# Attention's eight gated rows in two seven-product units, and w_o's first two rows split by operand

## The chip, the cores and the metric

The kernel runs on one core of a Trainium2 chip. The metric is device time in microseconds (us): the median of three runs of the kernel before is 2486.24 us (2486.18 to 2487.11). The engines are named as the profile names them: PE is TensorE (PEld its weight loads), DVE is VectorE, ACT is ScalarE, POOL is GpSimd, SP is SyncE, which here only issues DMAs. Each engine works through its own queue in order and waits at an instruction until what it needs is there.

## The reference

Two layers of an encoder trunk over 640 tokens (512 new ones, and 8 running streams of 16), width 1024. Each layer is a half feed-forward step, a mixer, and another half feed-forward step. The change touches the end of the mixer:

```python
g = jax.nn.sigmoid(g + b_gate)                 # 2 x 1024 gate columns of z = h @ w_in
g_conv, g_attn = jnp.split(g, 2, axis=-1)
y_conv, conv_new = _short_conv(cb, cc, cv, conv_prev, w_conv)      # 512 channels
y_attn, k_new, v_new = attn_fn(q, k, v)                            # 512 channels
m = g_conv * (y_conv @ w_conv_out) + g_attn * (y_attn @ w_attn_out)
return m @ w_o, conv_new, k_new, v_new         # added to x
```

`w_conv_out` and `w_attn_out` are 512 x 1024, `w_o` is 1024 x 1024. All of it is float32.

## The kernel before

Tensors lie transposed: 128 channels on the partitions, 640 tokens along the free side, in two halves of 320 (t1, t2). A "row" is 128 output channels. Every float32 product is made of three matmuls of a rounded type: an operand is split into a high part, cast by ACT, and a low part, the rest, subtracted by DVE (`whi`/`wlo` for weights, names ending in `hi`/`lo` for data); the matmuls are high x high, high x low, low x high.

Two ways of multiplying occur. The plain way (`product`, L448, `multiply`, L430): for each row, each 128-channel block of the input and each token half, three matmuls of 128 x 320. The seven-product way: input blocks are taken in even and odd pairs, and the output in two rows r and two token halves, so that a 2 x 2 by 2 x 2 block product needs seven products instead of eight, of mixed weights and mixed data. The data kinds are X11, X21, X22 (a block as it is) and T5, T7, N6, T4 (sums and differences of blocks); the weight kinds come from two slabs of 1024 columns and sums of their halves. The order is always X11, X21, N6, T5, T7, X22, T4, and N6, T7 and T4 add onto PSUM tile `a`, which is copied out between.

Weights come as 512 KB slabs from HBM on SP's queue, in the order that `mixer_order` (L115) writes, into three `raw` buffers. `source` (L301) makes a slab's mixed weights on DVE, `prep` (L350) issues the high casts on ACT two slabs ahead, `flush` (L366) the low subtractions on DVE; `slab` (L373) takes the next one, `quiet` takes it without preparing. A seven-product unit uses four such entries, from two slabs. For the third of them the sum of two halves is added by a DMA pair on POOL (`lend_one`, L277, tile `one`).

`outputs` (L1485) is the stage in question. PE, DVE and ACT run exactly in the order in which the code is written here (`manual_schedule`). It has:
- `gate_pair(m, at)` (L1506), "gates m": two gate rows by seven, 84 matmuls. `at` holds three places at which extra work of DVE and ACT can be put: before product X21, before T7 and before X22. The sigmoids are left to the next unit (`lates`, issued by `due`).
- `out(m, y)` (L1551): one plain row, 24 matmuls, then gating, and for attention rows the addition to `mm`.
- `rows(name, ms, y)` (L1617), "rows co": four rows by seven, 84 matmuls, with the gating in seven steps on DVE and the copies s1, s2, s5 out of PSUM on ACT. It is used for convolution rows 4 to 7.
- `mixed` (L1583) makes the mixtures of one pair of y blocks in place and splits them.

The order in a layer is gates 2, convolution rows 0 to 3 plain, gates 4, gates 6, rows co, and then four times: one gate pair (8, 10, 12, 14) and two plain attention rows (the products `py` from `ya`). `give` splits the merged rows m into high and low as operands of w_o, which follows: eight plain rows `po` of 48 matmuls, each added to x and passed to `ex.final`, which prepares the next feed-forward step.

PSUM has two accumulators of two banks (`acc`) and four of one bank (`att`) in this stage. Gate tiles come from a pool of four (`tmp`).

Of the kernel before, what the change touches and what calls it, by code (L numbers as in the profile page):

```python
# [126 lines left out]

# [66 lines left out]
def trunk(ctx: ExitStack, tc: tile.TileContext, xin, wst, small, pbias, samplebias, kcache, vcache, gfin,  # L196
# [24 lines left out]
    def acc(name):  # L221
        return banks["acc"].tile([P, 2, 512], F32, tag="acc", name=name)
# [7 lines left out]
    def tmp(name):  # L230
        return tp.tile([P, UW], F32, tag="t", name=name)[:, :T]

    def split(hi, lo, src):
        ACT.copy(hi, src)
        DVE.tensor_tensor(out=lo, in0=src, in1=hi.bitcast(F32), op=ALU.subtract)
# [1097 lines left out]
    def mixer(l, after):  # L1333
# [151 lines left out]
    def outputs(l, gp, X, st, cs, ycp, yas, sigmoid, gates):  # L1485
# [15 lines left out]
        def due():  # L1501
            for f in lates:
                f()
            lates.clear()

        def gate_pair(m, at):  # L1506
            n = f"{l}_{m}"
            pa, pb, pc = (att(f"q{i}{n}")[:, :HT] for i in "abc")
            u, g = gates[m], gates[m + 1] = tmp(f"g{n}"), tmp(f"g{n}_1")
            s0 = quiet()  # L1510
            block(pa, s0, 0, X11, every, True, True)
            ACT.copy(c1, pa)
# [9 lines left out]
            ACT.copy(u2, pa)  # L1522
# [42 lines left out]
            if post:  # L1565
                post()

        yc, ya, mo = [], [], []
        more = []
        yas_ = [yas[:, c, :] for c in range(CT)]  # L1570
# [5 lines left out]
        def give(ms):  # L1576
            for m in ms:
                mo.append(parts(hp, "h", f"m{l}_{m}", mm[m]))
# [4 lines left out]
        def mixed(i, y, z):  # L1583

            z = z.rearrange("p c (a b) -> p (c a) b", a=2)
            e1, e2, o1, o2 = (z[:, i] for i in range(4))
            add(e1, e1, e2, ALU.subtract)
            add(e2, o2, e2, ALU.subtract)
            for out, a in ((o2, e1), (o1, o2)):
                DVE.scalar_tensor_tensor(out=out, in0=a, scalar=-1.0, in1=out, op0=ALU.mult, op1=ALU.subtract)  # L1590
            yield
            hi, lo = (gp.tile([P, 3, HT], F32R, tag=f"x{i}{p}", name=f"x{p}{l}_{len(more)}") for p in ("hi", "lo"))
            ACT.copy(hi, z[:, 1:])
            more.append((hi, lo))
            yield
            low(lo, z[:, 1:], hi)
            yield
            hi, lo = (u[:, t2] for u in y[2 * i])
            ACT.copy(hi, e1)
            yield  # L1600
            low(lo, e1, hi)
            yield

        def take_even(c, src):
            y = tuple(gp.tile([P, T], F32R, tag=f"y{c}{i}", name=f"ya{l}_{c}{i}") for i in ("hi", "lo"))
            split(*(z[:, t1] for z in y), src[:, t1])
            ya.append(y)

        EXTRA = XT7, XT4, XN6

        def kind(y, i, k):
            if k in EXTRA:
                return tuple(z[:, EXTRA.index(k)] for z in more[i - 2])
            hi, lo = y[2 * i + (k in (X21, X22))]
            return tuple(z[:, t2 if k in (X22, XT5) else t1] for z in (hi, lo))

        def rows(name, ms, y, then=None):  # L1617

            n = f"{name}{l}_{ms[0]}"
            gs = [gates[m + (KT if name == "ao" else 0)] for m in ms]  # L1620
# [5 lines left out]
            def mul(ps, s, half, k, start):  # L1626
                for u in range(2):
                    for i in range(2):
                        kp = half * NP + 2 * u + i
                        wh, wl = (z[:, kp * P : (kp + 1) * P] for z in s)  # L1630
                        xh, xl = kind(y, i, k)
                        for j, (w, x_) in enumerate(((wh, xh), (wh, xl), (wl, xh))):
                            PE.matmul(ps[u], w, x_, start=start and i == 0 and j == 0,
                                      stop=i == 1 and j == 2, skip_group_check=True)
# [24 lines left out]
            mul(a, w, 0, XN6, False)  # L1659
            ACT.copy(s2, two(A))  # L1660
            gated(0, [s1[:, u] for u in range(2)], t1)
            mul(c, w, 1, XT5, True)
            for u in range(2):
                ACT.copy(s5[:, u], c[u])
# [11 lines left out]
            if then:  # L1676
                then()
# [8 lines left out]
        def total(m0, m1):  # L1686
            for m in range(m0, m1):
                add(mm[m], mm[m], gates[KT + m])

        none = lambda: None  # L1690

        def also(*fs):
            return lambda: [f() for f in fs]

        def going(z):
            return lambda: next(z)

        gate_pair(2, [none, none, lambda: take(yc, "yc", range(CT), ycs)])
        z = [mixed(i, yc, ycp[i]) for i in range(2)]
        out(0, yc, None, going(z[0]))  # L1700
        out(1, yc, None, also(going(z[0]), going(z[1])))
        out(2, yc, None, also(going(z[0]), going(z[1])))
        out(3, yc, None, going(z[1]))
        both = also(going(z[0]), going(z[1]))
        gate_pair(4, [both, both, none])
# [665 lines left out]
```

## Time and profile before

| | |
|---|---|
| median of 3 runs | 2486.24 us |
| profiled execution | 2487.08 us |
| its span, first to last instruction | 2485.3 us |
| PE busy | 2471.0 us, 99% |
| DVE busy | 2158.3 us, 87% |
| ACT busy | 1373.0 us, 55% |
| POOL busy | 317.4 us, 13% |
| granted clock of PE | 0.999 |

A row of the time-ordered view has start and duration in us, engine, source line, operation, tiles written and read, shapes and count; in brackets, how long the engine stood idle before it and what it waited for. Matmuls are pipelined, so a matmul lasts 0.31 us in such a row while the next starts 0.15 us later: the pace is read from starts. The same holds for DVE and ACT, whose next instruction starts up to 0.1 us before the last one's end if it does not need its result. A row of the waits has the waiting engine, tile and line, the releaser, the time in total, the number of waits, and the longest. Layer 0's gates, rows and w_o lie at about 635 to 833 us of the span, layer 1's at about 1867 to 2065 us.

### The profile page before, as it was taken

The page shows a single profiled execution, that of the slowest core. Times are in us where ns is not written, and L with a number is a line of the kernel's source. Part 1 is how long each engine was busy: PE and PEld are TensorE (multiplying, and loading weights), DVE is VectorE, ACT ScalarE, POOL GpSimd, SP SyncE. Part 2 cuts the span into 40 slices and gives each one's busy share as a digit, 9 for nine tenths or more (in the row PEclk, how much of TensorE's full clock was granted, in tenths as well). Part 3 has the DMA queues.
Part 4 walks back from the last instruction along what each step waited for, and adds up shares of the span by engine and source line. Part 5 has one row for each costly group of instructions (what it writes and reads, how often), then busy time and mean ns, then how long its engine had stood idle before and what let it go on. Part 6 is the DMA issues. An engine that isn't in the chain of part 4 may idle for free.

```text
span 2485.3 us, 43991 instructions
## 1 busy us (share of the span) xinstructions
PE 2471.0 (99%) x17288; PEld 2418.2 (97%) x17288; DVE 2158.3 (87%) x3587; ACT 1373.0 (55%) x2196; POOL 317.4 (13%) x479
## 2 busy tenths in 40 slices
PE   9999999999999999999999999999999999999999
PEld 8999999889999999999999999998999999999998
DVE  7999998888886899998799999988878769999997
ACT  6555556665554555555665555556645455555555
POOL 0111112211000001111001111121110000111111
PEclk9999999999999999999999999999999999999999
DMA  4443445335343334444334443453453333443444
GB/s 155 126 118 102 123 119 121 113 109 177 104 118 108 94 101 106 112 117 120 108 94 109 110 118 102 116 128 107 132 173 92 115 111 89 107 116 106 113 117 117
DMA packets 113072, 287.11 MB, mean 116 GB/s; under 512 B 12928, under 2 KB 52480, under 8 KB 112864
## 3 DMA queue, kind: packets, MB, share of 16 engines
q1 hardware_dynamic: 69552, 220.10, 28.0%
q0 software_dynamic: 42880, 63.94, 13.7%
q8 instruction: 135, 2.21, 0.4%
q14 instruction: 73, 0.60, 0.1%
q10 hardware_dynamic: 432, 0.25, 0.0%
HBM read 238.43 MB, written 7.94 MB: 99 GB/s over the span
## 4 chain that ended last, share of the span: by engine, by line
PE 92%; DVE 4%; ACT 2%; DMA 1%; issue 1%; SPq 0%; DVEq 0%; ACTq 0%; POOLq 0%
PE pab L458 12%; PE paa L458 11%; PE pcb L458 6%; PE daa L1143 6%; PE pca L458 5%; PE dab L1143 5%; PE po L434 5%; PE qa L458 4%; PE py L434 3%; PE pbb L458 3%; PE dca L1143 3%; PE pba L458 3%; PE dcb L1143 2%; PE ma_qk L458 2%; PE ma_cv L458 2%; PE pv L1770 2%
## 5 line engine op out<-in xcount | busy, mean ns | idle before, releaser
L363 ACT CAST whi<-raw 128x512 fp32r<-128x512 f32 (+1 forms) x573 | 500.4, 878 | 371.3 <-PE pbb L458 46.0
L368 DVE TENSOR_TENSOR wlo<-raw,whi 128x512 fp32r<-128x512 f32 (+1 forms) x573 | 574.4, 1005 | 135.9 <-ACT whi L363 132.1
L363 ACT CAST whi<-s 128x1024 fp32r<-128x1024 f32 (+1 forms) x160 | 151.6, 947 | 313.3 <-issue 111.4
L458 PE MATMUL pab<-xhib,whi 128*128 128x320 f32 x704 | 217.5, 309 | 0.0
L458 PE MATMUL pab<-xlob,whi 128*128 128x320 f32 x704 | 217.0, 308 | 0.0
L458 PE MATMUL pab<-xhib,wlo 128*128 128x320 f32 x704 | 217.0, 308 | 0.0
L458 PE MATMUL paa<-xhia,whi 128*128 128x320 f32 x640 | 197.7, 309 | 0.2 <-DVE ga L295 0.2
L458 PE MATMUL paa<-xhia,wlo 128*128 128x320 f32 x640 | 197.5, 309 | 0.0
L458 PE MATMUL paa<-xloa,whi 128*128 128x320 f32 x640 | 197.4, 308 | 0.0
L368 DVE TENSOR_TENSOR wlo<-s,whi 128x1024 fp32r<-128x1024 f32 (+1 forms) x160 | 174.8, 1092 | 4.6 <-ACT whi L363 4.6
L1165 POOL DMA_DIRECT2D x<-c_a x80 | 70.0, 1022 | 573.8 <-ACT ahia L1047 205.5
L1165 POOL DMA_DIRECT2D x<-c_b x72 | 62.8, 1002 | 583.6 <-ACT ahib L1047 205.8
L458 PEld LDWEIGHTS pab<-xhib,whi 128*128 128x128 f32 x704 | 132.1, 188 | 0.9 <-issue 0.9
L458 PEld LDWEIGHTS pab<-xlob,whi 128*128 128x128 f32 x704 | 132.2, 188 | 0.0
L458 PEld LDWEIGHTS pab<-xhib,wlo 128*128 128x128 f32 x704 | 132.1, 188 | 0.0
L458 PEld LDWEIGHTS paa<-xhia,whi 128*128 128x128 f32 x640 | 120.1, 188 | 1.1 <-DVE ga L295 0.5
L458 PEld LDWEIGHTS paa<-xloa,whi 128*128 128x128 f32 x640 | 120.1, 188 | 0.2 <-DVE xloa L702 0.2
L458 PEld LDWEIGHTS paa<-xhia,wlo 128*128 128x128 f32 x640 | 120.1, 188 | 0.2
L295 DVE TENSOR_TENSOR raw<-s,raw 128x512 f32<-128x512 f32 x160 | 109.1, 682 | 0.0
L458 PE MATMUL pcb<-xhib,wlo 128*128 128x320 f32 x352 | 108.7, 309 | 0.0
L458 PE MATMUL pcb<-xlob,whi 128*128 128x320 f32 x352 | 108.5, 308 | 0.0
L458 PE MATMUL pcb<-xhib,whi 128*128 128x320 f32 x352 | 108.5, 308 | 0.0
(840 smaller groups left out, 8150.4 us busy)
## 6 DMA issues: line engine op xcount, KB each, us to landing
raw<-in_wst SPq DMA_DIRECT2D x375, 512.0 KB, 3.6
x<-c_a POOLq DMA_DIRECT2D x80, 160.0 KB, 4.6
x<-c_b POOLq DMA_DIRECT2D x72, 160.0 KB, 3.6
lent<-in_wst POOLq DMA_DIRECT2D x36, 256.0 KB, 3.9
kc<-in_kcache SPq DMA_DIRECT2D x32, 256.0 KB, 5.2
vc<-in_vcache SPq DMA_DIRECT2D x16, 512.0 KB, 4.8
one<-in_wst POOLq DMA_DIRECT2D x28, 256.0 KB, 4.1
x<-u_a POOLq DMA_DIRECT2D x40, 160.0 KB, 4.1
```

The costliest lines, as they stand in the source:

```text
L295: DVE.tensor_tensor(out=out, in0=a, in1=b, op=op)
L363: ACT.copy(hi[:, d], src[:, c])
L368: DVE.tensor_tensor(out=lo, in0=src, in1=hi.bitcast(F32), op=ALU.subtract)
L434: PE.matmul(ps[:, a, :HT], w, x[a] if isinstance(x, tuple) else x[:, a * HT : (a + 1) * HT], start=first and j == 0 and not seeded, stop=l ...
L458: PE.matmul(ps, a, b, start=start and kp == 0 and j == 0, stop=stop and kp == NP - 1 and j == 2, skip_group_check=True)
L1143: PE.matmul(ps[u], w, y, start=start and i == 0 and j == 0, stop=i == 1 and j == 2, skip_group_check=True)
L1165: POOL.dma_start(x[ms[2 * u + r]][:, cols], z[:, u], accum_op=ALU.add)
L1770: PE.matmul(pv[t], xx[:, t * P : (t + 1) * P], w[:, kk * AW : (kk + 1) * AW], start=c == 0 and kk == 0 and j == 0, stop=c == KT // 2 - 1 a ...
```

## The change

- The eight attention rows are made by two calls of `rows`, one after gates 8 and 10 (attention rows 0 to 3), one after gates 12 and 14 (rows 4 to 7). The order of the weight stream follows.
- For that, the mixtures of both pairs of y blocks are made at once, on 640 columns, by `mix(0)` to `mix(3)` inside gates 10. Their high and low parts are issued by `high` and `rest`: T5 and N6's high part inside gates 10; N6's low part, T7 and T4 inside the first attention `rows`, at three places: `first` (before product X21), `mid` (before T5) and `late` (before X22).
- y's high and low parts are made inside gates 8, in its second and third place.
- `rows` no longer copies convolution rows 4 and 5 to `mm` at its end; both copies go to gates 8 (`lates` and `moves`). Gate tiles are taken a little later in `gate_pair`.
- The attention rows stay in their gate tiles, and `total` adds them to `mm` on DVE, 640 columns each: four inside gates 12, four at the end. `given` splits m0 and m2 inside gates 14, m1 and m3 inside the second `rows`, m4 to m7 at the end.
- w_o's rows 0 and 1 are multiplied together: first both with operands 0, 2, 1, 3, then each with operands 4 to 7. Their two slabs of weights are taken at once.

```diff
-    for i in range(4):
-        out += [gates[4 + i], ("ao", 2 * i), ("ao", 2 * i + 1)]
+    for i in range(2):
+        out += gates[4 + 2 * i : 6 + 2 * i] + [("rows", ("ao", tuple(range(4 * i, 4 * i + 4))))]
...
             hold[0] = True
+            first = [acc(f"po{l}_{m}") for m in range(2)]
+            ws = [[tiles.take() for _ in mo] for _ in first]
+            for ks in ((0, 2, 1, 3), range(KT // 2, KT)):
+                for p, w in zip(first, ws):
+                    for k in ks:
+                        multiply(p, w[k], mo[k], k == 0, k == KT - 1)
             for m in range(KT):
-                po = acc(f"po{l}_{m}")
-                product(po, mo)
+                po = first[m] if m < 2 else acc(f"po{l}_{m}")
+                if m > 1:
+                    product(po, mo)
...
-            u, g = gates[m], gates[m + 1] = tmp(f"g{n}"), tmp(f"g{n}_1")
             s0 = quiet()
             block(pa, s0, 0, X11, every, True, True)
             ACT.copy(c1, pa)
             due()
+            u, g = gates[m], gates[m + 1] = tmp(f"g{n}"), tmp(f"g{n}_1")
...
+        def take_even(c):
+            y = tuple(gp.tile([P, T], F32R, tag=f"y{c}{i}", name=f"ya{l}_{c}{i}") for i in ("hi", "lo"))
+            split(*(z[:, t1] for z in y), srcs[c][:, t1])
+            ya.append(y)
...
+        def minus(out, a):
+            DVE.scalar_tensor_tensor(out=out, in0=a, scalar=-1.0, in1=out, op0=ALU.mult, op1=ALU.subtract)
...
+        za = yas.rearrange("p (i c) (a b) -> p i (c a) b", i=2, a=2)
+
+        def mix(n):
+
+            e1, e2, o1, o2 = (za[:, :, k] for k in range(4))
+            if n == 0:
+                add(e1, e1, e2, ALU.subtract)
+            elif n == 1:
+                add(e2, o2, e2, ALU.subtract)
+            else:
+                minus(*((o2, e1) if n == 2 else (o1, o2)))
+
+        def place(k):
+            if k == XT5:
+                return [(*(u[:, t2] for u in ya[2 * i]), za[:, i, 0]) for i in range(2)]
+            c = EXTRA.index(k)
+            return [(*(u[:, :, c] for u in x["ao"]), za[:, :, 1 + c])]
+
+        def high(*ks):
+            for k in ks:
+                for hi, _, z in place(k):
+                    ACT.copy(hi, z)
+
+        def rest(*ks):
+            for k in ks:
+                for hi, lo, z in place(k):
+                    low(lo, z, hi)
...
-        def rows(name, ms, y, then=None):
+        def rows(name, ms, first, mid=None, late=None, end=False):
...
             due()
             prep(used[0] + 1)
             flush()
+            if first:
+                first()
             mul(b, w, 1, X21, True)
...
             ACT.copy(s2, two(A))
             gated(0, [s1[:, u] for u in range(2)], t1)
+            if mid:
+                mid()
             mul(c, w, 1, XT5, True)
...
             flush()
             ahead()
             gated(1, [s5[:, u] for u in range(2)], t2, -1.0)
+            if late:
+                late()
             mul(c, w, 1, X22, False)
...
-            if name == "co":
-                moved(0)
             mul(a, w, 0, XT4, False)
-            flush()
+            if not end:
+                flush()
             gated(1, a, t1, -1.0)
             if name == "co":
-                lates.append(lambda: moved(1))
+                lates.append(lambda: moved(0))
+                moves.append(lambda: moved(1))
+            if end:
+                flush()
...
-        rows("co", (4, 5, 6, 7), yc)
-        for m in range(KT, 2 * KT, 2):
-            last = m == 2 * KT - 2
-            gate_pair(m, [none, none, (lambda: take(ya, "ya", range(CT), yas_)) if m == KT else
-                          (lambda: give(range(1))) if last else none])
-            out(m, ya, (lambda: give(range(1, 4))) if last else None)
-            out(m + 1, ya, (lambda: give(range(4, 6))) if last else None)
-        give(range(6, KT))
+        rows("co", (4, 5, 6, 7), None)
+        gate_pair(8, [lambda: moves[0](), lambda: (take_even(0), take(ya, "ya", [1], srcs)),
+                      lambda: (take_even(2), take(ya, "ya", [3], srcs))])
+        room("ao")
+        gate_pair(10, [lambda: (mix(0), mix(1)), lambda: (mix(2), high(XT5)),
+                       lambda: (mix(3), rest(XT5), high(XN6))])
+        rows("ao", (0, 1, 2, 3), lambda: rest(XN6), lambda: (high(XT7), rest(XT7)), lambda: (high(XT4), rest(XT4)))
+        gate_pair(12, [lambda: total(0, 1), none, lambda: total(2, 3)])
+        gate_pair(14, [none, lambda: (begun(*range(4)), given(0, 2)), none])
+        rows("ao", (4, 5, 6, 7), None, lambda: given(1, 3), None, True)
+        begun(*range(4, KT))
+        total(4, 5)
+        given(4)
+        total(6, 7)
+        given(5, 6, 7)
```

More of the change, by code (lines that the diff above doesn't have):

```diff
@@ L1566, in out @@
                 post()
-        yc, ya, mo = [], [], []
-        more = []
-        yas_ = [yas[:, c, :] for c in range(CT)]
+        yc, ya = [], []
+        mo = [None] * KT
+        srcs = [yas[:, c, :] for c in range(CT)]
+        x, moves = {}, []
         def take(y, name, cs, srcs):
@@ L1574, in take, with room, mixed @@
                 y.append(parts(gp, f"y{c}", f"{name}{l}_{c}", srcs[c]))
-        def give(ms):
-            for m in ms:
-                mo.append(parts(hp, "h", f"m{l}_{m}", mm[m]))
+        def take_even(c):
+            y = tuple(gp.tile([P, T], F32R, tag=f"y{c}{i}", name=f"ya{l}_{c}{i}") for i in ("hi", "lo"))
+            split(*(z[:, t1] for z in y), srcs[c][:, t1])
+            ya.append(y)
         def low(lo, z, hi):
             DVE.tensor_tensor(out=lo, in0=z, in1=hi.bitcast(F32), op=ALU.subtract)
-        def mixed(i, y, z):
-            z = z.rearrange("p c (a b) -> p (c a) b", a=2)
-            e1, e2, o1, o2 = (z[:, i] for i in range(4))
+        def room(name):
+            x[name] = tuple(gp.tile([P, 2, 3, HT], F32R, tag=f"x{i}", name=f"x{i}{name}{l}") for i in ("hi", "lo"))
+        def minus(out, a):
+            DVE.scalar_tensor_tensor(out=out, in0=a, scalar=-1.0, in1=out, op0=ALU.mult, op1=ALU.subtract)
+        def mixed(i):
+            z = ycp[i].rearrange("p c (a b) -> p (c a) b", a=2)
+            e1, e2, o1, o2 = (z[:, k] for k in range(4))
             add(e1, e1, e2, ALU.subtract)
             add(e2, o2, e2, ALU.subtract)
-            for out, a in ((o2, e1), (o1, o2)):
-                DVE.scalar_tensor_tensor(out=out, in0=a, scalar=-1.0, in1=out, op0=ALU.mult, op1=ALU.subtract)
+            minus(o2, e1)
+            minus(o1, o2)
             yield
-            hi, lo = (gp.tile([P, 3, HT], F32R, tag=f"x{i}{p}", name=f"x{p}{l}_{len(more)}") for p in ("hi", "lo"))
+            hi, lo = (u[:, i] for u in x["co"])
             ACT.copy(hi, z[:, 1:])
-            more.append((hi, lo))
             yield
@@ L1597, in mixed @@
             yield
-            hi, lo = (u[:, t2] for u in y[2 * i])
+            hi, lo = (u[:, t2] for u in yc[2 * i])
             ACT.copy(hi, e1)
@@ L1602, in mixed, with kind @@
             yield
[L1604 to L1607, printed above, removed]
+        za = yas.rearrange("p (i c) (a b) -> p i (c a) b", i=2, a=2)
[20 more added lines that the diff above has]
+                    low(lo, z, hi)
         EXTRA = XT7, XT4, XN6
-        def kind(y, i, k):
+        def kind(name, i, k):
             if k in EXTRA:
-                return tuple(z[:, EXTRA.index(k)] for z in more[i - 2])
-            hi, lo = y[2 * i + (k in (X21, X22))]
+                return tuple(z[:, i, EXTRA.index(k)] for z in x[name])
+            hi, lo = (yc if name == "co" else ya)[2 * i + (k in (X21, X22))]
             return tuple(z[:, t2 if k in (X22, XT5) else t1] for z in (hi, lo))
-        def rows(name, ms, y, then=None):
+        def rows(name, ms, first, mid=None, late=None, end=False):
             n = f"{name}{l}_{ms[0]}"
@@ L1630, in mul @@
                         wh, wl = (z[:, kp * P : (kp + 1) * P] for z in s)
-                        xh, xl = kind(y, i, k)
+                        xh, xl = kind(name, i, k)
                         for j, (w, x_) in enumerate(((wh, xh), (wh, xl), (wl, xh))):
@@ L1690, in outputs, with total, begun, given @@
+            if end:
+                flush()
+        def total(*ms):
+            for m in ms:
+                add(mm[m], mm[m], gates[KT + m])
+        def begun(*ms):
+            for m in ms:
+                mo[m] = tuple(hp.tile([P, T], F32R, tag=f"h{i}", name=f"m{l}_{m}{i}") for i in ("hi", "lo"))
+        def given(*ms):
+            for m in ms:
+                split(*mo[m], mm[m])
         none = lambda: None
[L1692 to L1696, printed above, removed]
+        def going(*zs):
+            return lambda: [next(z) for z in zs]
@@ L1698, in outputs @@
         gate_pair(2, [none, none, lambda: take(yc, "yc", range(CT), ycs)])
-        z = [mixed(i, yc, ycp[i]) for i in range(2)]
+        z = [mixed(i) for i in range(2)]
+        room("co")
         out(0, yc, None, going(z[0]))
-        out(1, yc, None, also(going(z[0]), going(z[1])))
-        out(2, yc, None, also(going(z[0]), going(z[1])))
+        out(1, yc, None, going(*z))
+        out(2, yc, None, going(*z))
         out(3, yc, None, going(z[1]))
-        both = also(going(z[0]), going(z[1]))
@@ L1705, in outputs @@
-        gate_pair(4, [both, both, none])
+        gate_pair(4, [going(*z), going(*z), none])
         gate_pair(6, [none] * 3)
-        rows("co", (4, 5, 6, 7), yc)
-        for m in range(KT, 2 * KT, 2):
-            last = m == 2 * KT - 2
-            gate_pair(m, [none, none, (lambda: take(ya, "ya", range(CT), yas_)) if m == KT else
-                          (lambda: give(range(1))) if last else none])
-            out(m, ya, (lambda: give(range(1, 4))) if last else None)
-            out(m + 1, ya, (lambda: give(range(4, 6))) if last else None)
```

4 lines of the change are left out of this document (removed).

## The prediction, made before the change was run

> **What bounds the kernel now.** I read the page's busy times first, then the waits of TensorE's weight loads in the stage that the change touches, then the three queues side by side in order of time. The page:
>
> ```profile
> span 2485.3 us, 43991 instructions
> PE 2471.0 (99%) x17288; PEld 2418.2 (97%) x17288; DVE 2158.3 (87%) x3587; ACT 1373.0 (55%) x2196; POOL 317.4 (13%) x479
> ```
>
> TensorE is busy for all but 14.3 us of the span: fewer matmuls save their own time, and every wait added to TensorE's queue is lost. The waits of layer 0's gate, row and w_o stage (640 to 800 us):
>
> ```profile
> PEld qa L458 <- ACT capsm L1512: 0.4, 1, 0.4
> PEld po L434 <- issue: 0.3, 1, 0.3
> PEld po L434 <- DVE m_6lo L235: 0.2, 1, 0.2
> ```
>
> There is almost nothing here to win back but matmuls. The pace, from the first matmuls of four units (rows co, gates 8, the two attention products 8 and 9, gates 10):
>
> ```profile
> 686.40 0.31 PE L1633 MATMUL raco<-yc_0hi,whi 128*128 128x320 f32 x1
> ...
> 698.72 0.31 PE L458 MATMUL qa<-hhim,whi 128*128 128x320 f32 x1
> ...
> 711.46 0.45 PE L434 MATMUL py<-ya_0hi,whi 128*128 128x320 f32 x2
> ...
> 718.50 0.31 PE L458 MATMUL qa<-hhim,whi 128*128 128x320 f32 x1
> ```
>
> A by-seven row unit is 84 matmuls in 12.32 us, 0.1467 us each (1.76 us per product of 12). Two plain attention products are 48 matmuls in 7.04 us, the same pace.
>
> VectorE is the engine to watch, by the stretch view (columns: length, then PE, PEld, DVE, ACT, POOL busy) of the row unit and of the gate unit 10:
>
> ```profile
> 686.40:698.72 12.32, 12.32 (x86) 12.32 (x85) 10.31 (x18) 7.23 (x12) 1.43 (x2) 1.00 0.49 129
> 718.50:730.82 12.32, 12.32 (x87) 12.32 (x86) 9.37 (x15) 5.12 (x9) 1.42 (x2) 1.00 0.49 131
> ```
>
> **The change, part by part.** *Matmuls.* Per layer, eight plain attention rows are 8 x 24 = 192 matmuls; two row units are 168. Saved: 24 x 0.1467 = 3.52 us a layer, 7.04 us in all. This is certain and is all on the path.
>
> *VectorE's load.* The six units from gates 8 to the second row unit take 6 x 12.32 = 73.9 us of TensorE. VectorE has 4 x 9.37 + 2 x 10.31 = 58.1 us from the two rows above, and in addition, at the start-to-start times of the rows below (0.74 for 640 columns, 710.29 to 711.03; 0.40 for 320, 0.88 for two with 0.48 for the last): splitting y, 2.3; four `mix` steps and T5, 3.8; the low parts of N6, T7, T4, 2.2; `total`, 4 x 0.74; four low parts of m, 3.0. Sum 72.4 of 73.9 us, so it has room only where nothing holds it, and its queue runs in written order. What matters is where the three low parts stand in that queue.
>
> VectorE's rows over gates 6 and rows co, where the same code runs today:
>
> ```profile
> 683.16 0.49 DVE L295 TENSOR_TENSOR g<-qa,c 128x320 f32<-128x320 f32 x1 [2.39 <-PE qa L458]
> ...
> 689.42 0.68 DVE L295 TENSOR_TENSOR raw<-s,raw 128x512 f32<-128x512 f32 x1
> 691.08 0.69 DVE L368 TENSOR_TENSOR wlo<-one,whi 128x512 fp32r<-128x512 f32 x1 [0.98 <-ACT whi L363]
> 691.69 0.69 DVE L368 TENSOR_TENSOR wlo<-raw,whi 128x512 fp32r<-128x512 f32 x1
> 692.30 0.82 DVE L295 TENSOR_TENSOR capsm<-rbco,capsm 128x640 f32<-128x640 f32 x1
> ...
> 695.47 0.82 DVE L295 TENSOR_TENSOR rs<-raco,rs 128x640 f32<-128x640 f32 x1 [0.96 <-PE raco L1633]
> 696.21 1.22 DVE L368 TENSOR_TENSOR wlo<-raw,whi 128x1024 fp32r<-128x1024 f32 x1
> ...
> 698.67 0.89 DVE L1642 SCALAR_TENSOR_TENSOR g<-rs,g 128x320 f32<-128x320 f32 x2
> 699.48 0.88 DVE L295 TENSOR_TENSOR rs<-rcco,rs 128x320 f32<-128x320 f32 x2
> ...
> 703.08 0.68 DVE L295 TENSOR_TENSOR raw<-s,raw 128x512 f32<-128x512 f32 x1
> ...
> 710.29 0.82 DVE L235 TENSOR_TENSOR ya_0lo<-ya,ya_0hi 128x640 fp32r<-128x640 f32 x1
> 711.03 0.82 DVE L235 TENSOR_TENSOR ya_1lo<-ya,ya_1hi 128x640 fp32r<-128x640 f32 x1
> ```
>
> and TensorE's second matmuls of N6, T7 and T4 in that unit, the first that read a low part:
>
> ```profile
> 690.07 0.31 PE L1633 MATMUL raco<-xlo,whi 128*128 128x320 f32 x1
> ...
> 693.59 0.31 PE L1633 MATMUL raco<-xlo,whi 128*128 128x320 f32 x1
> ...
> 697.11 0.31 PE L1633 MATMUL raco<-xlo,whi 128*128 128x320 f32 x1
> ```
>
> *N6's low part* (`first`) is written behind the second `flush`, so where the row of 692.30 begins. Started there it ends at 692.30 + 0.82 + 0.03 = 693.15, and TensorE wants it at 690.07: a wait of 3.1. Gates 10 puts `mix(3)` (0.74) and T5's two low parts (0.80) in front, behind the wait of 683.16. The sum of 689.42 moves by 1.54 to 690.96, ends at 691.65, its high part (0.62 on ACT) at 692.30, the low part of `raw` starts at 692.33 instead of 691.69, and N6's ends at 693.78: a wait of 3.7. The idle 2.39 us at 683.16 is spent by `mix(0)` to `mix(2)` (0.74 + 0.85 + 0.74, the second waiting for the first), and gates 8 hands on some lateness, up to 0.4: 4.1. Ends 3.1 and 4.1; I take 3.9, between the last two.
>
> *T7's low part* (`mid`) waits for ACT:
>
> ```profile
> 692.00 0.69 ACT L1660 COPY rs<-raco 128x640 f32<-128x640 f32 x1
> 692.76 0.43 ACT L1664 COPY rs<-rcco 128x320 f32<-128x320 f32 x1
> ```
>
> The copy of `a` starts at 692.00; T7's high part follows at its 640-column spacing of 0.63 and takes 0.72, to 693.38; the low part ends at 694.23 against 693.59: 0.6 late. In today's rows the two multiplies of 693.6 would push it to 1.7; behind N6's wait they are long done, so 0.6.
>
> *T4's low part* (`late`) stands behind the row of 698.67, so where 699.48 begins; it ends at 700.33. T4 wants it at 697.11: a wait of 3.2. Nothing can pull it forward: the chain hangs on T7's own end (695.47: add, weight low part, two sums, two multiplies), and TensorE has only product 22 to do in that time.
>
> *Gates 8.* The copies `moved` go behind c1, two of them in front of c1's successor u2. Today:
>
> ```profile
> 700.79 1.35 ACT L1647 COPY yc<-g 128x640 f32<-128x640 f32 x2 [0.78 <-DVE g L1640]
> 702.05 0.41 ACT L1512 COPY capsm<-qa 128x320 f32<-128x320 f32 x1
> ...
> 705.62 0.41 ACT L1522 COPY capsm<-qa 128x320 f32<-128x320 f32 x1
> ```
>
> c1 at 702.05, behind the copies, makes the wait of 0.4 seen above; that goes. But ACT then does c1, two copies, the two casts of third weights (the second needs the sum of 703.08, which ends at 703.8), the other two copies (1.26), a cast (0.52), and u2 ends near 706.5, where product T7 would start at 705.8: 0.7 late. Net +0.3.
>
> *The other units.* Four `total` (3.0) and the m splits go under gates 12, 14 and the second row unit, whose VectorE sums (12.3, 10.9, 11.8) fit in 12.32 each; the 7.7 us of waits just before let it catch up. At nothing; without that cover, gates 12 would wait up to 0.5.
>
> *w_o.* After the last T4 product VectorE does two multiplies (0.8), a 1024 low part (1.13), two totals (1.48) and m4's low part: 4.6 us with the read latency, and TensorE reaches row 4 after 48 matmuls, 7.0 us. m5, m6, m7 end near 7.6, 8.4, 9.1 and are wanted at 8.2, 9.1, 10.0. So no wait, by under a microsecond; the 0.2 + 0.2 us of today's start (issue, m_6lo) go, of which I count 0.2. The two first slabs taken together hold ACT until product 0 ends; nobody waits for what is queued there before product 3.
>
> *Loads and buffers.* The eight rows' weights stay four slabs a layer on SP's queue; POOL issues four more `one` transfers a layer, where it is 13% busy. Rows co runs today with the same transfers beside it, and TensorE waits for none: nothing. Gate units back to back take turns in the same four one-bank accumulators as gates 4 and 6 do today, without a wait in the list above; gates 12 and 14 write their u and g where gates 8 to 11 lay, which `total` has read by then, ahead on VectorE's own queue.
>
> **Sum** per layer: -3.52 + 3.9 + 0.6 + 3.2 + 0.3 - 0.2 = +4.3; two layers +8.6. The profiled execution took 2487.08 us (span 2485.3 and 1.8 around it), so 2495.7; it stood 0.84 above the median of the runs, 2486.24, which gives 2494.8.
>
> **The clock.** TensorE's pace behind the one long idle stretch in this trace, the 5.60 us at the start:
>
> ```profile
> 5.60 0.63 PE L434 MATMUL poa<-xhia,whi 128*128 128x320 f32 x1 [5.60 <-ACT whi L758]
> ...
> 10.03 0.47 PE L434 MATMUL poa<-xhia,wlo 128*128 128x320 f32 x1
> 10.30 0.47 PE L434 MATMUL poa<-x2hia,wlo 128*128 128x320 f32 x1
> ...
> 11.61 0.31 PE L434 MATMUL poa<-xhia,whi 128*128 128x320 f32 x1
> ```
>
> 0.267 us a matmul for 5.0 us, then 0.147: a loss of 5.0 x (1 - 0.147/0.267) = 2.2 us. The page's granted clock does not show this stretch, and the next longest wait of a weight load is 0.9 us, so waits of 3 to 4 us lie between what the trace knows:
>
> ```profile
> PEclk9999999999999999999999999999999999999999
> ...
> PEld qa L458 <- ACT ya L1988: 0.9, 1, 0.9
> ```
>
> [...]
>
> **The rivals.** (1) *The slow stretch returns.* After N6's wait in both layers 2 x 2.2, less T7's 2 x 0.6 that slower matmuls swallow: +3.2, 2498.0; after T4's too, 2502.4. For it: the rows above. Against: the known case is 5.6 us long. (2) *VectorE bounds the whole stage*: 72.4 of 73.9 us, and it stood idle 0.98 and 0.96 us in a single unit waiting on ACT and PE; if 2 us a layer of this come back in gates 12, 14 or w_o, 2498.8. Against: the first row unit's waits feed it. (3) *N6's and T4's waits half as long*, if the mixing of gates 10 finds more room: 2 x 2 us less, 2491. Against: T4's chain is fixed. (4) *Faster*: VectorE takes the three low parts when their high parts are there, not in written order. Then no wait, -7.04 - 0.2 x 2: 2478.8. It decides only if N6's and T4's both come 3 us sooner; every VectorE row of rows co stands in written order, which speaks against it. With all costs at their ends on the light side (3.1, 0.6, 3.2, 0.0) a layer is still +3.2.
>
> **How the numbers follow.** My forecast, three waits at full clock, 0.56; (1) 0.17, (2) 0.11, (3) 0.10, (4) 0.06. A measurement tells 0.2%, 5 us, from no change: 2481.3 to 2491.2 is same. Forecast, (1), (2) and about 0.06 of (3) are slower, 0.90; the rest of (3) is same, 0.04; (4) is faster. The forecast alone spans 2492.6 (3.1 at N6, nothing in gates 8) to 2496.2 (4.1, and 0.5 in gates 12). The range goes from (3), 2490.5, to most of (1) and (2), 2501; (4) and the upper half of (1) are left out, some 0.15.
>
> **What would show it.** TensorE has 48 matmuls fewer. In each layer its first attention row unit takes about 20 us instead of 12.3, with weight loads waiting for VectorE's subtraction in `rest` three times: near 3.9, 0.6, 3.2 us. Gates 8 waits once for ACT, 0.7. Matmuls behind the waits keep 0.147. Wrong if the row unit takes 12.3 us, if the pace there is 0.27, or if waits lie in gates 12, 14 or w_o.

## The result, and the profile after

The changed kernel takes 2505.56 us (median; 2504.24 to 2505.81) against 2486.39 us beside it: a ratio of 1.0076, 95% interval 1.0063 to 1.0088. It is slower, as forecast, but by 19.2 us where 8.6 were forecast, and outside the range. The profiled execution took 2504.24 us.

The page after (span, busy times, granted clock):

```profile
span 2502.5 us, 44044 instructions
...
PE 2472.2 (99%) x17240; PEld 2417.0 (97%) x17240; DVE 2193.4 (88%) x3665; ACT 1392.2 (56%) x2238; POOL 323.3 (13%) x487
...
PEclk9999999999999999999999999999999899999999
```

PE has 48 matmuls fewer (17288 to 17240), 7.04 us of work at 0.1467, and yet is busy 1.2 us longer. The granted clock has an 8 that was not there: in that slice, which holds layer 1's attention rows, PE ran slower.

The waits of PE in the whole kernel (columns: total, times, longest):

```profile
PE raao L1670 <- DVE xloao L1590: 14.0, 4, 4.0
...
PE po L434 <- DVE m_5lo L235: 1.5, 2, 0.8
PE qa L458 <- ACT capsm L1529: 1.3, 2, 0.7
```

The waits for low parts (`raao`, `xloao`) are those foreseen. `m_5lo` is new and was not. PE in order of time, layer 0 and then layer 1, at the two long waits of the first attention row unit (start, duration; idle before in brackets):

```profile
732.36 0.41 PE L1670 MATMUL raao<-xloao,whi 128*128 128x320 f32 x1 [3.90 <-DVE xloao L1590]
...
733.10 0.47 PE L1670 MATMUL raao<-xloao,whi 128*128 128x320 f32 x1
733.37 0.47 PE L1670 MATMUL raao<-xhiao,wlo 128*128 128x320 f32 x1
...
744.57 0.41 PE L1670 MATMUL raao<-xloao,whi 128*128 128x320 f32 x1 [3.08 <-DVE xloao L1590]
744.82 0.31 PE L1670 MATMUL raao<-xhiao,wlo 128*128 128x320 f32 x1
744.97 0.31 PE L1670 MATMUL raao<-xhiao,whi 128*128 128x320 f32 x1
```

```profile
1970.15 0.63 PE L1670 MATMUL raao<-xloao,whi 128*128 128x320 f32 x1 [3.95 <-DVE xloao L1590]
1970.58 0.47 PE L1670 MATMUL raao<-xhiao,wlo 128*128 128x320 f32 x1
1970.85 0.47 PE L1670 MATMUL raao<-xhiao,whi 128*128 128x320 f32 x1
...
1982.77 0.64 PE L1670 MATMUL raao<-xloao,whi 128*128 128x320 f32 x1 [3.08 <-DVE xloao L1590]
1983.20 0.47 PE L1670 MATMUL raao<-xhiao,wlo 128*128 128x320 f32 x1
1983.47 0.47 PE L1670 MATMUL raao<-xhiao,whi 128*128 128x320 f32 x1
```

The waits have the lengths forecast, 3.9 and 3.1. Read the pace from the starts behind them: 0.27 us a matmul (733.10 to 733.37, 1970.58 to 1970.85) in place of 0.147. Only behind layer 0's second wait is it 0.15 at once. So the same wait of 3.08 us is followed by full pace in layer 0 and by half pace in layer 1.

The granted clock shows the difference. It is 0.50 from 732.64 to 736.05 us in layer 0, and from 1968.27 to 1975.09 and 1981.92 to 1988.75 us in layer 1; all these edges lie a whole number of 3.413 us apart. The stretch view over such steps at T4's wait, two of layer 0 and three of layer 1 (length, then PE, PEld, DVE, ACT and POOL busy; then the granted clock):

```profile
739.47:742.88 3.41, 2.02 (x14) 1.76 (x12) 3.15 (x4) 0.09 (x1) 0.00 (x0) 1.00 0.00 0
742.88:746.29 3.41, 1.72 (x11) 1.72 (x12) 3.41 (x9) 1.14 (x2) 0.00 (x0) 1.00 0.00 0
...
1978.51:1981.92 3.41, 1.18 (x9) 0.91 (x7) 3.38 (x7) 0.64 (x2) 0.00 (x0) 1.00 0.00 0
1981.92:1985.33 3.41, 2.56 (x9) 2.57 (x10) 3.41 (x8) 0.50 (x1) 0.00 (x0) 0.50 0.02 5
1985.33:1988.75 3.42, 3.42 (x14) 3.42 (x14) 1.67 (x4) 0.00 (x0) 0.00 (x0) 0.50 0.00 0
```

In layer 0 the wait is shared by two steps, with 1.39 and 1.69 us idle; in layer 1, 2.23 us of it fall into one step, and the clock is halved from the next.

The row unit's length by the same view, layer 0 with all units from gates 8 to the end of w_o:

```profile
699.09:712.32 13.23, 12.58 (x86) 12.31 (x85) 11.95 (x23) 9.31 (x17) 1.44 (x2) 1.00 0.48 134
...
724.62:746.30 21.68, 14.66 (x87) 13.87 (x85) 17.11 (x30) 9.81 (x16) 1.43 (x2) 0.92 0.31 82
...
783.59:840.95 57.36, 56.58 (x386) 56.32 (x385) 44.77 (x63) 29.14 (x37) 2.88 (x4) 1.00 0.33 102
sum 141.86, PE 133.38 PEld 131.76 DVE 118.61 ACT 77.02 POOL 8.62; mean PE 19.05 PEld 18.82 DVE 16.94 ACT 11.00 POOL 1.23
```

The same stretch before, and layer 1's after:

```profile
sum 134.58, PE 134.40 PEld 133.69 DVE 101.32 ACT 67.65 POOL 5.74; mean PE 26.88 PEld 26.74 DVE 20.26 ACT 13.53 POOL 1.15
```

```profile
sum 145.04, PE 136.54 PEld 135.15 DVE 118.71 ACT 77.14 POOL 8.65; mean PE 34.14 PEld 33.79 DVE 29.68 ACT 19.28 POOL 2.16
```

Layer 1 took 134.59 us before. The stage grew by 7.28 and 10.45, together 17.7 us; the span grew by 17.2, so all of the change lies here.

### The profile page after: what moved, and what is told of

It is laid out like the page before. It is cut to its first block, busy times and chain, and to the rows that moved or that the text cites. A ratio compares the mean times of both kernels' runs of the same rounds, so it can differ in the third digit from the quotient of the medians.

```text
span 2502.5 us, 44044 instructions
## 1 busy us (share of the span) xinstructions
PE 2472.2 (99%) x17240; PEld 2417.0 (97%) x17240; DVE 2193.4 (88%) x3665; ACT 1392.2 (56%) x2238; POOL 323.3 (13%) x487
## 4 chain that ended last, share of the span: by engine, by line
PE 89%; DVE 6%; ACT 2%; issue 1%; DMA 1%; SPq 0%; DVEq 0%; ACTq 0%; POOLq 0%
PE pab L458 12%; PE paa L458 11%; PE pcb L458 6%; PE pca L458 5%; PE daa L1143 5%; PE dab L1143 5%; PE po L434 4%; PE qa L458 3%; PE pbb L458 3%; PE pba L458 3%; PE dca L1143 3%; PE dcb L1143 2%; PE ma_cv L458 2%; PE ma_qk L458 2%; PE pv L1825 2%; DVE wlo L368 2%
```

## The experiments

My theory after seeing this: three losses stand apart from each other, the waits at low parts that are late in VectorE's queue, the half pace behind them, and small waits in gates 8, gates 14 and w_o. A rival for the size: VectorE's load bounds the stage, whatever waits where. Another for the pace: it has a cause of its own and only happens to fall there. All diffs are against the changed kernel. The kernel before stood at 2486.7 us (2486.65 to 2486.77) beside all of them.

**Without the three low parts.**

```diff
                         xh, xl = kind(name, i, k)
+                        if name == "ao" and ms[0] == 0 and k in EXTRA:
+                            xl = xh
```

> The changed kernel, but in the first attention row unit of each layer the matmuls that read the low parts of N6, T7 and T4 read the high parts instead: that unit leaves the low parts of three mixtures out of its result, VectorE still makes them, and no matmul there waits for them. My theory (the three waits of 4.1, 0.3 and 3.2 us a layer, and behind them stretches at half pace, cost the time): all of these go, and the time falls from 2505.6 by 15.2 for the waits and by some 7 for the half pace, to 2482 to 2486, below the kernel before. Rival A (VectorE bounds the whole stage, with 72 of 74 us of work, and the waits only stand where the queue happens to be late): TensorE waits as long at other tiles, and the time stays above 2495. Rival B (the half pace comes from elsewhere than the waits): half-pace matmuls stay in the trace.

Measured 2486.54 us, ratio 0.9998 (0.9989 to 1.0008). So the three waits and the half pace are worth 19 us, the whole loss; the granted clock is 1.00 in the whole stage, so the half pace went with the waits. But this kernel has 7 us less matmul work and no long wait, and is only level with the kernel before, just above the range expected. Its stretches in layer 0, gates 10, first rows, gates 12 and 14:

```profile
711.77:724.06 12.29, 12.29 (x86) 12.29 (x85) 12.09 (x21) 7.91 (x14) 1.43 (x2) 1.00 0.41 123
724.06:737.49 13.43, 12.88 (x86) 12.35 (x85) 13.29 (x22) 8.49 (x14) 1.43 (x2) 1.00 0.48 121
737.49:750.50 13.01, 12.84 (x87) 12.31 (x85) 12.83 (x24) 4.93 (x9) 1.43 (x2) 1.00 0.38 110
750.50:763.32 12.82, 12.58 (x87) 12.32 (x85) 11.60 (x19) 7.73 (x13) 0.00 (x0) 1.00 0.38 105
```

VectorE's busy time (fourth number) is 12.1 of 12.3, 13.3 of 13.4, 12.8 of 13.0: it is full, and PE waits in the last three for weights' low parts, 0.46, 0.16 and 0.24 us in one piece and less in others. That is the rival of a bound on VectorE, and it is real once the long waits are gone: 1.1 + 0.7 us over 12.3 in the rows and gates 12. In gates 14 VectorE is busy for 11.60 of 12.82 us, so the 0.5 us over 12.3 there is not shown to be load.

**T4's parts earlier**, at `mid` behind T7's.

```diff
-... lambda: (high(XT7), rest(XT7)), lambda: (high(XT4), rest(XT4)))
+... lambda: (high(XT7), rest(XT7), high(XT4), rest(XT4)))
```

> T4's high and low part are issued in the second place of the first attention row unit, behind T7's, instead of in the third. My theory: VectorE stands idle there for about 1 us before the sum of T7's product, so the low part costs nothing, T4's wait of 3.2 us a layer is gone, and with it the half pace behind it; N6's wait of 4.1 and the half pace behind that stay. 2505.6 - 6.5 - 0 to 5: 2494 to 2499. Rival A (VectorE as the bound): the same wait comes back one or two products later, 2503 to 2506.

Measured 2496.2 us (2494.14 to 2497.07), ratio 1.0034 (1.0021 to 1.0048). T4's waits are gone (`raao` waits 7.9 us in all, two times), and 9.4 us with them, where the two waits alone are 6.5 (3.24 each: 3.08 idle, and the time until the matmul then starts). The rest, 2.9 us, is about what the half pace behind layer 1's T4 wait costs in the changed kernel, 2.8 us by its starts. The prediction's "Nothing can pull it forward" held only for the place `late`; the data were ready earlier.

**Matmuls with low parts last** in those rows' products (the other eight of the twelve first).

> In the first attention row unit each product of 12 matmuls first issues the eight that need no low part of the data and then the four that do; nothing else changes. My theory: each wait becomes shorter by the 7 matmuls that now lie ahead of it, about 1 us, so about 3.0 and 2.2 instead of 4.1 and 3.2, and T7's goes: 2.3 us a layer less. If a wait must last over 3.4 us or so to bring the half pace, that goes in all places: 2505.6 - 4.6 - 7, 2493 to 2496. If any wait of 2 us and more brings it (rival), only the waits shrink: 2499 to 2502.

Measured 2499.49 us, ratio 1.0049 (1.0034 to 1.0064), with executions between 2496.16 and 2502.92. The waits fell to 2.0 us, as they should, and the half pace stayed in three of four places:

```profile
1969.24 1.43 PE L1673 MATMUL raao<-xloao,whi 128*128 128x320 f32 x4 [2.02 <-DVE xloao L1590]
1970.47 0.47 PE L1673 MATMUL rcao<-ya_0hi,whi 128*128 128x320 f32 x1
1970.74 0.47 PE L1673 MATMUL rcao<-ya_0hi,wlo 128*128 128x320 f32 x1
...
1980.10 0.86 PE L1673 MATMUL raao<-xloao,whi 128*128 128x320 f32 x4 [2.06 <-DVE xloao L1590]
1980.79 0.31 PE L458 MATMUL qa<-hhim,whi 128*128 128x320 f32 x1
1980.94 0.31 PE L458 MATMUL qa<-hlom,whi 128*128 128x320 f32 x1
```

2.02 us, then half pace; 2.06 us, then full pace. My expectation, that a wait must last over 3.4 us or so to bring the half pace, was wrong; the rival expectation held. In steps of 3.413 us as above, the wait of 2.06 us that brought none falls as 1.37 and 0.68 us into two of them.

**Spare matmuls in the waits.** 25 ahead of N6's product and 20 ahead of T4's, into PSUM that is overwritten or no longer read.

```diff
+        FILL = {XN6: (1, 25), XT4: (0, 20)}
...
                 for u in range(2):
+                    if name == "ao" and ms[0] == 0 and u == 0 and k in FILL:
+                        wh, xh = s[0][:, half * NP * P : (half * NP + 1) * P], kind(name, 0, k)[0]
+                        for _ in range(FILL[k][1]):
+                            PE.matmul((c if FILL[k][0] else b)[0], wh, xh, start=True, stop=True, ...)
```

> The changed kernel with 25 spare matmuls on TensorE just ahead of N6's product in the first attention rows, and 20 ahead of T4's (at 0.147 us: 3.7 and 2.9 us). They write a bank that is overwritten or no longer read, so the output is unchanged and the wait for the low parts is filled with work instead of idling. In the changed kernel's trace the two waits are 3.9 to 4.0 and 3.1 us, and matmuls behind them go at 0.26 us for a while: about 1.6 us lost in layer 0 and 5.1 in layer 1. Theory (the slow pace comes from TensorE standing idle, and is apart from the wait itself): the slow pace goes, the time on the path stays; 2505.6 - 6.7 = 2499 us, 2497 to 2501. Rival (the slow pace is brought by something else in that stage, such as transfers or the load of the other engines): the slow pace stays, 2504 to 2507 us.

Measured 2499.0 us (2498.5 to 2499.86), ratio 1.0048 (1.0033 to 1.0063). The same place as in the changed kernel at 732.36, N6's low part in layer 0:

```profile
732.03 0.41 PE L1675 MATMUL raao<-xloao,whi 128*128 128x320 f32 x1 [0.24 <-DVE xloao L1590]
732.28 0.31 PE L1675 MATMUL raao<-xhiao,wlo 128*128 128x320 f32 x1
732.43 0.31 PE L1675 MATMUL raao<-xhiao,whi 128*128 128x320 f32 x1
```

The low part is as late as ever, work that nobody needs stands where PE idled, and the kernel is 6.6 us faster: the half pace is brought by idling, not by the stage. This separates the two losses: 6.6 us of pace, and 12.6 us that waits and queues cost beyond what the saved matmuls give back.

**Fewer spare matmuls**: `FILL = {XN6: (1, 16), XT4: (0, 15)}`.

> The run with spare matmuls ahead of N6's and T4's products, with 16 of them at N6 instead of 25 and 15 at T4 instead of 20, so that TensorE idles about 0.24 + 9 x 0.147 = 1.6 us at N6 and 0.36 + 5 x 0.147 = 1.1 us at T4. The path is otherwise as long as with all spare matmuls (2499.0 us). Waits of 2.0 us brought the slow pace in three of four places, waits up to 0.8 us never. If a stand of 1.1 or 1.6 us brings it too, a slow stretch of 3.4 us costs 1.5 to 1.7 us each: 2500.5 to 2506 us, with half pace behind the waits. If not: 2498 to 2500 us at full pace throughout.

Measured 2498.56 us (2498.32 to 2499.3), ratio 1.0048 (1.0034 to 1.0062).

```profile
732.09 0.41 PE L1675 MATMUL raao<-xloao,whi 128*128 128x320 f32 x1 [1.56 <-DVE xloao L1590]
732.35 0.31 PE L1675 MATMUL raao<-xhiao,wlo 128*128 128x320 f32 x1
732.50 0.31 PE L1675 MATMUL raao<-xhiao,whi 128*128 128x320 f32 x1
```

Idle stretches of 1.56 (N6) and 0.88 us (T4) in both layers, and full pace behind all of them.

**w_o's rows 0 and 1 one after the other**, as before the change (the whole block `first`, `ws`, `multiply` left out).

> The changed kernel with w_o's rows 0 and 1 multiplied one after the other as before, all else as changed. My theory: the low parts of m4 to m7 are ready as in the changed kernel, but row 0 wants m4 after 24 matmuls (3.5 us) instead of 48 (7.0), so the wait for m5 of 0.8 us grows to 3 to 4 us a layer, spread over m4 to m7: 2505.6 + 5 to 6, 2510 to 2512. Rival (the order in w_o hides nothing, VectorE's later queue sets the end of w_o in both): 2504 to 2507.

Measured 2513.9 us (2512.34 to 2514.83), ratio 1.0105 (1.0088 to 1.0122). Splitting the rows by operand is worth 8.3 us in the changed kernel, 2 us more than the upper end of my expectation, which had no half pace in w_o. Plain rows reach m4 too early:

```profile
791.52 0.56 PE L434 MATMUL po<-m_4hi,whi 128*128 128x320 f32 x2 [1.41 <-ACT m_4hi L234]
792.38 0.56 PE L434 MATMUL po<-m_4lo,whi 128*128 128x320 f32 x2 [0.30 <-DVE m_4lo L235]
794.59 0.90 PE L434 MATMUL po<-m_5lo,whi 128*128 128x320 f32 x2 [1.06 <-DVE m_5lo L235]
```

Three waits within 4.5 us, none over 1.41, and the last row's 0.90 in place of 0.56 shows half pace as well: the granted clock of this w_o is 0.95. So it is not one stand alone that counts here, but how much of a few microseconds PE stood: 1.41, 0.30 and 1.06 us of 4.5.

**Two small queue orders**: m5 split ahead of m6's and m7's totals; `moves[0]` from gates 8's first place to its third.

> The changed kernel with two small reorderings and nothing else: w_o's m5 is split ahead of the totals of m6 and m7 instead of behind them, and the copies of the last channel rows (moves[0]) go from the first to the third place of gates 8, behind the splits of y. Theory: the two waits of the changed kernel go, 0.78 us for m5's low part and 0.65 us for u2's copy, in each layer; 2505.6 - 2 x 1.4 = 2502.8 us, 2501.5 to 2504. Rival (the queues behind are as late, so that m6 or gates 10 wait instead): 2505 to 2506.5 us.

Measured 2504.57 us (2504.18 to 2505.81), ratio 1.0071 (1.0056 to 1.0086): between the two expectations. Both waits are gone, and others came: m6's parts wait 0.21 and 0.30 us, gates 10 waits 0.3. The half pace blurs the rest, since it falls differently from execution to execution: the run with low parts last took 2496.16 us at a granted clock of 0.998 and 2502.92 us at 0.996.

**The mixtures earlier on VectorE**, the same instructions, with those two orders.

```diff
-        gate_pair(8, [lambda: moves[0](), lambda: (take_even(0), take(ya, "ya", [1], srcs)),
-                      lambda: (take_even(2), take(ya, "ya", [3], srcs))])
+        gate_pair(8, [lambda: take_even(0), lambda: (take(ya, "ya", [1], srcs), take_even(2)),
+                      lambda: (take(ya, "ya", [3], srcs), mix(0), moves[0]())])
...
-        gate_pair(10, [lambda: (mix(0), mix(1)), lambda: (mix(2), high(XT5)),
-                       lambda: (mix(3), rest(XT5), high(XN6))])
-        rows("ao", (0, 1, 2, 3), lambda: rest(XN6), lambda: (high(XT7), rest(XT7)), lambda: (high(XT4), rest(XT4)))
+        gate_pair(10, [lambda: (mix(1), mix(2)), lambda: (high(XT5, XN6), rest(XT5)),
+                       lambda: (rest(XN6), high(XT7))])
+        rows("ao", (0, 1, 2, 3), lambda: (mix(3), rest(XT7)), lambda: (high(XT4), rest(XT4)))
```

> The two reorderings of the run before, and the mixtures issued earlier on VectorE, all with the same instructions: y's splits at the three places of gates 8, mixture 0 behind them, mixtures 1 and 2 at gates 10's first place, T5's and N6's high parts and T5's low at its second, N6's low and T7's high at its third; mixture 3 and T7's low inside the rows' first product, T4's parts behind N6's. Theory (the cost is the place of the low parts in VectorE's queue, not VectorE's load): no wait over 1 us and no slow pace; the kernel without low parts came to 2486.5, and the small waits for m5 and u2 go too, 2 x 1.4, while waits of 0.2 to 0.7 us at some products remain; 2482 us, 2480 to 2486. Rival (VectorE's work bounds the stage, so that what is done earlier makes the weights' low parts late): 2487 to 2495 us.

Measured 2484.81 us (2484.19 to 2486.63), ratio 0.9992 (0.9983 to 1.0002): 20.7 us of the changed kernel's time, by order alone. N6's low part, from VectorE's rows in time order:

```profile
725.14 0.82 DVE L1590 TENSOR_TENSOR xloao<-ya,xhiao 128x640 fp32r<-128x640 f32 x1
```

PE wants it at 728.17 here. In the changed kernel the same instruction stands at

```profile
731.48 0.82 DVE L1590 TENSOR_TENSOR xloao<-ya,xhiao 128x640 fp32r<-128x640 f32 x1
```

though its high part had been ready since 722.56. No wait in the stage is over 0.5 us any more, and the pace is full throughout (granted clock 1.000 in the profiled execution).

**The same with the four mixtures on GpSimd** (`POOL.tensor_tensor`, all four at gates 8's third place; T4's high part stands one place earlier in the rows).

> As the run before, but the four mixtures of both pairs run on GpSimd, all at the third place of gates 8 (N6's is kept with the other sign and turned in its two parts), so that VectorE has 4 x 0.8 = 3.3 us less to do in gates 10 and the first rows of each layer. Theory (behind the place in the queue, VectorE's load is the next bound): 1 to 2 us per layer better than with the mixtures on VectorE; 2479 us, 2477 to 2483. Rival (GpSimd's adds take several times VectorE's 0.8 us, or hold back the weights' transfers that it issues): no better than the run before, or slower, 2483 to 2500 us.

Measured 2494.62 us, ratio 1.0033 (1.0021 to 1.0046), 10 us slower than on VectorE. VectorE and GpSimd at that place:

```profile
708.93 2.56 DVE L1536 TENSOR_TENSOR g<-g,rrm 128x320 f32<-128x320 f32 x1
711.41 2.56 DVE L368 TENSOR_TENSOR wlo<-raw,whi 128x1024 fp32r<-128x1024 f32 x1
```

```profile
709.25 1.88 POOL L1625 TENSOR_TENSOR ya<-ya 128x640 f32<-128x640 f32 x1
711.21 1.68 POOL L1627 TENSOR_TENSOR ya<-ya 128x640 f32<-128x640 f32 x1
```

The rival expectation held. GpSimd needs 1.7 to 1.9 us for what VectorE does in 0.8; that alone was no harm, since PE waits for no mixture. But VectorE's multiply of 320 columns, 0.49 us elsewhere, takes 2.56, and the low part of 1024 columns 2.56 in place of 1.22. Each lasts about as long as the GpSimd add beside it and its own work together (1.88 + 0.49 = 2.4 us, 1.68 + 1.22 = 2.9). VectorE's busy time rose from 2192.7 to 2198.1 us although eight mixtures of 0.82 us had left it. PE then waits 2.29 us (layer 0) and 2.92 us (layer 1) for weights' low parts in gates 10, where the run above waits 0.41, and half pace follows both waits (in layer 0 the granted clock of gates 10 is 0.90). The rows do not show what holds VectorE there, nor which of the two engines was first (the multiply is recorded from 708.93, the add from 709.25).

**Two more orders on top of the mixtures on VectorE**: T7's low part ahead of mixture 3, and w_o's row 2 prepared later.

```diff
-            ws = [[tiles.take() for _ in mo] for _ in first]
+            ws = [[tiles.take() for _ in mo]]
+            second = quiet()
+            ws.append([tuple(c[:, k * P : (k + 1) * P] for c in second) for k in range(KT)])
...
-... lambda: (mix(3), rest(XT7)), ...
+... lambda: (rest(XT7), mix(3)), ...
```

> The run with the mixtures issued earlier on VectorE, and two more reorderings of it: T7's low part stands ahead of mixture 3 instead of behind it (it was 0.42 us late, and a wait costs about 0.27 us more until the next matmul starts), and the low part of the weights of w_o's row 2 (1.13 us on VectorE) no longer stands ahead of m4's and m5's, since row 1's slab is taken without preparing another (m6's two parts were 0.22 and 0.30 us late). Theory (what is left over is the order in VectorE's queue): 0.7 us at T7 and 1.06 us at w_o go in each layer; 2484.8 - 3.5 = 2481.3 us, 2480 to 2483. Rival (VectorE has no room, so that T4's low part or row 2 and 3 of w_o wait instead): 2484 to 2487 us.

Measured 2482.87 us (2482.39 to 2484.52), ratio 0.9986 (0.9977 to 0.9995): faster than both kernels, by 3.8 us than the one before. Its waits of PE in the stage, and its first attention rows and w_o:

```profile
PE raao L1672 <- DVE rs L295: 1.0, 2, 0.5
PE qa L458 <- DVE wlo L368: 0.9, 3, 0.4
```

```profile
724.13:737.44 13.31, 12.81 (x86) 12.34 (x85) 13.14 (x21) 7.96 (x13) 1.43 (x2) 1.00 0.50 133
...
775.13:831.50 56.37, 56.37 (x386) 56.33 (x385) 44.95 (x63) 29.02 (x37) 2.87 (x4) 1.00 0.36 103
```

w_o is back at 56.37 us; T7's wait is gone, and T4's first matmul now waits 0.5 for `rs`, held up in VectorE's queue by T4's own low part and mixture 3. 1.6 of the 3.5 us expected did not come: VectorE, busy 13.14 of 13.31 us in the rows, has no more room there. Of the 3.52 us of matmuls a layer, 1.9 arrive.

## Why the prediction was right and wrong

The direction and the mechanism of the waits were right: 48 matmuls fewer, and three low parts that stand too late in VectorE's written order. What failed is the pace behind the waits.

- *Matmuls*, -3.52 a layer: as forecast.
- *N6*, +3.9: idle 3.90 and 3.95, and the matmul starts 4.07 and 4.19 us late.
- *T4*, +3.2: idle 3.08, 3.24 us late, in both layers.
- *T7*, +0.6: 0.30 in layer 0, nothing in layer 1, where slow matmuls before it swallowed it, as the rival on the clock said.
- *Gates 8*, +0.3: 13.23 in place of 12.74, +0.49.
- *Gates 12 and 14*, nothing: +0.3 a layer, a weight's low part at N6's product in gates 14. A small miss.
- *w_o*, "no wait, by under a microsecond", and 0.2 gained: wrong. m5's low part is 0.78 us late and w_o takes 57.36 us in place of 56.55; 0.2 is gained at its start. What the sum of the queue left out is the low part of row 2's weights (1.13 us), which stands ahead of m4's; the last experiment moved it away, with m5 split earlier, and got the time back.
- *The clock*, nothing: this is the term that failed. The forecast took the three waits at full clock with a chance of 0.56 and the return of the slow stretch at 0.17 ("Matmuls behind the waits keep 0.147"). The half pace came; from the starts behind the waits, against 0.147 each, it costs 1.6 us in layer 0 and 5.1 in layer 1. That is 6.7 of the 9.1 us by which the stage's growth of 17.7 us exceeds the forecast 8.6; the run with spare matmuls measured it as 6.6. Without the half pace that run takes 2499.0 us, inside the range and 4 us above the forecast: mostly w_o, gates 8 and gates 14. The first rival, with T4's wait too, gave 2502.4, 3 us under the median.

The argument against that rival was that the known slow stretch followed 5.6 us of idling and these waits are shorter. That was an argument from one length only; a wait of 2.02 us turned out to be enough, in the run with low parts last.

The rival of VectorE's bound had its size right (72.4 us forecast for the six units, 73.8 busy in layer 0 of the changed kernel) and was hidden: with 7 us of waits ahead, VectorE caught up in the other units. It appeared in the runs without those waits, where it takes back about half of what the matmuls save, or more. The rival that ended faster needed N6's and T4's parts 3 us sooner. VectorE did not do that of itself, as the prediction argued (N6's low part ran at 731.48, its high part ready since 722.56); a different written order does it, and the kernel is then faster.

## What to carry to other kernels

A wait on a busy TensorE had two prices here, the wait and the pace behind it: where 1.98 us or more were lost within one step of 3.41 us, half pace followed, and in the changed kernel it cost from 1.6 us (N6's wait, layer 0) to 2.8 us (T4's, layer 1). So look at the pace behind each long wait, break it into shorter ones that do not fall within the same step (layer 0's 3.08 us, shared as 1.39 and 1.69, brought none), or give TensorE other work in it (spare matmuls, 6.6 us here). An operand's due time hangs on its place in an in-order queue, not on when its inputs are ready: here the same instructions in another order moved 22.7 us. And when a long wait is removed, ask which full engine had used it to catch up; it takes back part of the gain (here 1.1 us in the first rows, with VectorE busy for 13.29 of 13.43 us).

## What the runs showed of the hardware

- Half pace (0.267 us for 0.147) followed single waits of 3.9 us always, of 3.1 and 2.0 us in some places and not in others, of 2.3 and 2.9 us in the one place each that had them, and single waits up to 1.56 us never; it also followed three waits of 1.41, 0.30 and 1.06 us within 4.5 us. The granted clock in these traces shows the half in pieces of 3.41 or 6.83 us, that is in whole steps of 3.41: once 3.41 us in layer 0 of the changed kernel, twice 6.83 in layer 1. What tells the outcomes apart is how much TensorE loses within one step. Counted by the starts of its matmuls at 0.147 us each, over the stage in the traces of all runs: a step at full pace in which 1.98 us or more were lost (the least, in w_o of layer 1 with plain rows) is followed by half pace every time, one with 1.83 us or less (the most, at layer 0's T4 wait in the changed kernel) never. So the same wait of 3.08 us has two outcomes, as it falls over the steps. What a loss between 1.83 and 1.98 us brings, no run here shows.
- A wait costs TensorE about 0.3 us more than the idle time in its row: N6's matmul starts 4.07 us late for 3.90 us idle, and behind a wait the next start follows after 0.26 us even at full pace (732.09 to 732.35, in the run with fewer spare matmuls), where it is 0.147 otherwise.
- VectorE's instructions beside GpSimd adds of 1.7 to 1.9 us became 2 to 5 times as long (0.49 to 2.56, 1.22 to 2.56 us). Moving elementwise work there did not relieve VectorE here, it held it up: its busy time rose from 2192.7 to 2198.1 us.
